# Eight slabs of modulation weights between the expert stage and the second block

## The chip, the cores and the metric

The kernel runs on one core of a Trainium2 chip. A core has a matrix engine (TensorE, PE in the profile; its weight loads are PEld), a vector engine (VectorE, DVE), a scalar engine (ScalarE, ACT), a general one (GpSimd, POOL) and a synchronizing one (SyncE, SP), which issues the DMA transfers here. Each engine carries out its own stream of instructions in order; semaphores tie the streams together. The metric is device time in microseconds of one execution, the median over runs.

## The reference, cut to what matters

The first block (a mixer with four branches, a layer norm, sixteen experts of which two serve a token, a second layer norm) is followed by a second block of two layers. Each layer has three sublayers, and each of them is scaled, shifted and gated by a modulation that comes from one conditioning vector:

```python
cond = jax.nn.silu(c)
for i in range(DEPTH_2):
    mod = cond @ ada_w[i] + ada_b[i]
    sh0, sc0, g0, sh1, sc1, g1, sh2, sc2, g2 = jnp.split(mod, N_MOD, axis=-1)
    h = modulate(rmsnorm(x, pre_norm[i, 0]), sh0, sc0)
    y = swiglu(h, ffn_w_gate[i, 0], ffn_w_up[i, 0], ffn_w_down[i, 0])
    x = x + FFN_HALF * g0[:, None, :] * rmsnorm(y, post_norm[i, 0])
    h = modulate(rmsnorm(x, pre_norm[i, 1]), sh1, sc1)
    ...  # y = dsa_mixer(h, ...) for i = 0, diff_mixer(h, ...) for i = 1
    x = x + g1[:, None, :] * rmsnorm(y, post_norm[i, 1])
    h = modulate(rmsnorm(x, pre_norm[i, 2]), sh2, sc2)
    ...  # a second swiglu, gated by g2
```

The width is 1024, there are 256 tokens. `cond @ ada_w[i]` is a product of one row with a matrix of 1024 x 9216 in fp32, 36 MB for each layer: little arithmetic, much to fetch.

## The kernel before

**Order of the work.** The mixer ends near 415 us, its norm and the router near 440. The experts run in eight pairs (`moe`) to about 685. At their end stands `overflow`, code for a token count above the capacity, behind a `tc.If` (L1515): a branch that every engine comes to. After it two matmul groups scatter the last pair's outputs into the result banks `y` (L1463), and the second layer norm follows, one half of 128 tokens at a time: `layer_norm` (L1165) as `ln2(0)`, `prenorm` (L327), then `ln2(1)` and its `prenorm`. `ln2w` is the normalized half; eight transposes `xp` (L350) turn it, and `xTf` is the result. Then `second` runs six steps (layer i, sublayer v): FFN(0,0), DSA(0,1), FFN(0,2), FFN(1,0), diff(1,1), FFN(1,2). The second half's head overlaps the first half's matmuls.

**Weights.** The class `Weights` holds one fixed list of slabs of 1 MB (`plan`). `pump` issues their transfers on SP strictly in that order, each as soon as a buffer of a fitting tag is free; `_raw_tag` picks the tag, the one whose buffers came free longest ago. A "split" slab is cut into a high part (ACT, L125) and a low part (DVE, L126), each in eight instructions of 256 columns, and PE multiplies with both: three passes (L276 to L278). A "raw" slab is used as it came, as the experts' are and the first FFN's first two slabs (`y<-xTf,rex` at L1596). From `second` on four buffers hold arriving slabs (one `rex`, three `raw`). During the experts more buffers serve (`wex`, `whi`, `wlo`, `wez`, `wea`).

**Modulation slabs.** `second_slabs` puts "ada" slabs among the weights. A group (layer i, sublayer v) has twelve of them: three column parts s (shift, scale, gate) of four slabs c. When the list's turn comes, `Ada.side` works a slab in. If the group is marked "vec", DVE multiplies and adds it into `asum` (L2138, L2140), two instructions of 1024 columns, and after four slabs PE sums `asum` over its partitions with a column of ones (8 records). If not, PE takes the slab itself (`rowsum`, L2146): four matmuls for each of its two blocks of 128 rows, which the profile records as 16. `drain` copies the sums out of the bank `adacc` on DVE (`aev`, one buffer, L2160) and sends them to row tiles by four transfers on SP (`arow`, L2163).

Before the change FFN(0,0), FFN(0,2) and FFN(1,0) carry 16, 16 and 12 vec slabs, DSA and diff 8 slabs each that are not vec, FFN(1,2) none. In DSA the eight stand behind the seven input slabs and ahead of the output slabs `dsa_w_out`; in diff three stand among the twelve input slabs and five behind them.

**What orders the instructions.** The scheduler of the framework writes each engine's stream from dependences, program order and its own estimate of times; `behind(tc, chain)` keeps a piece of code after the named instructions. Fillers such as the slab sums so come into gaps of that estimate.

Of the kernel before, what the change touches and what calls it, by code (L numbers as in the profile page):

```python
# [11 lines left out]
F32 = mybir.dt.float32  # L12
# [7 lines left out]
P = 128  # L20
T = 256
D = 1024
KC = D // P
# [5 lines left out]
@contextmanager  # L29
def behind(tc, chain):  # L30
    with ExitStack() as c:
        for i in chain:
            c.enter_context(tc.issue_after(i))
        yield


class Weights:
# [24 lines left out]
        self.hist[tag] = []  # L62

    def _raw_tag(self, j):
        order = ("wey", "wex", "rex", "b4", "raw", "whi", "wlo", "wez", "wea", "x") if self.slabs[j][0] == "raw" else ("rex", "raw")
        if any(s[0] == "split" for s in self.slabs[self.next_split:j]):
            order = [t for t in order if t not in ("whi", "wlo")]
        return min((t for t in order if self.bufs[t]), key=self._age)
# [114 lines left out]
    def _take(self):  # L183
        i = self.pos
        self.pos += 1
        kind, parts, a, b = self.slabs[i][:4]
        self.n_used += kind == "split"
        self.low = max(self.low, i if self.held is None else self.held)
        self.pump()
        if kind == "split":  # L190
            return [q[:, :a * b].rearrange("p (a b) -> p a b", a=a) for q in self.split.pop(i)]
        t = self.raw.pop(i)
        if kind == "raw":
            t = t if isinstance(t, list) else [t[:, :a * b].rearrange("p (a b) -> p a b", a=a)]
            return [v[:, c] for v in t for c in range(v.shape[1])]
        return t[:, :a * b].rearrange("p (a b) -> p a b", a=a)


def interleave(main, side, a, b):
    out, n = [], 0  # L200
    for i, m in enumerate(main):
        out.append(m)
        while n < len(side) and i + 1 > a + (b - a) * n / len(side):
            out.append(side[n])
            n += 1
    return out + side[n:]
# [120 lines left out]
def prenorm(k, t, x, xn, scr):  # L327
    ss = sums(k)
    for j, js in enumerate(HALVES):
        square(k, x[:, t, js], scr, ss, j)  # L330
    return scaled(k, t, x, ss, xn)
# [1222 lines left out]
def ffn_slabs(wg, wu, wd):  # L1554
    out = []
    for f0 in range(0, LAST, 256):
        two = [cols_slab(wg, f0, f0 + 256), cols_slab(wu, f0, f0 + 256)]
        out += [keep(v) for v in two] if f0 == 0 else two
    g, u = (w.rearrange("(k p) n -> p k n", p=P) for w in (wg, wu))
    out.append(("split", [((0, KC, 0, P + HALF), g[:, :, LAST:]), ((0, KC, P + HALF, 2 * P), u[:, :, LAST + P:])], KC, 2 * P))  # L1560
    out.append(cols_slab(wu, LAST, LAST + P))
    for r0, r1 in down_order():
        out.append(rows_slab(wd, r0, r1))
    return out
# [141 lines left out]
def dsa_slabs(w_in, w_out):  # L1706
    return proj_slabs(w_in, [1536, 1280, 1024] + list(range(0, 1024, 256))) + [rows_slab(w_out, r, r + 256) for r in range(0, D, 256)]


def diff_slabs(w_in, w_out):  # L1710
    return proj_slabs(w_in, range(0, 3072, 256)) + [rows_slab(w_out, r, r + 256) for r in range(0, D, 256)]
# [348 lines left out]
NR = 3 * D // P  # L2060


class Ada:
# [41 lines left out]
        nc.scalar.activation(self.cond, self.cols[:, 96:104], AF.Silu)  # L2105

    def acc_tile(self, t):
        self.acc = t[:, :T]
        self.k.nc.vector.memset(self.acc, 0.0)

    def slabs(self, li, v, vec):
        self.order.append((li, v))
# [4 lines left out]
            out += [("ada", [((0, 2, 0, D), w[c, :, :, c0:c0 + D])], 2, D, (li, v, vec, s, c)) for c in range(KC // 2)]  # L2117
        return out

    def side(self, meta, raw):  # L2120
        nc = self.k.nc
        self.drain()
        li, v, vec, s, c = meta
        name = li, v
        if s == c == 0:
            self.rows[name] = self.pool.tile([NR, P], F32, name="arow", tag="arow", bufs=3)
            self.bias[name] = self.pool.tile([NR, P], F32, name="ab", tag="ab", bufs=3)
            nc.sync.dma_start(out=self.bias[name], in_=self.a["ada_b_2"][li].rearrange("(v r c) -> v r c", v=3, c=P)[v])
        if vec and c == 0:
            self.sum = self.k.hp.tile([P, D], F32, name="asum", tag="asum", bufs=1)  # L2130
        with behind(self.k.tc, self.k.W.after if vec else []):
            for q in range(2):
                kc = 2 * c + q
                cond = self.cond[:, kc:kc + 1]
                if not vec:
                    self.rowsum(cond, raw[:, q], kc == 0, kc == KC - 1)
                elif kc == 0:
                    nc.vector.tensor_scalar(self.sum, raw[:, q], cond, None, op0=OP.mult)  # L2138
                else:
                    nc.vector.scalar_tensor_tensor(self.sum, raw[:, q], cond, self.sum, op0=OP.mult, op1=OP.add)  # L2140
        if c == KC // 2 - 1:
            self.flush = name, s, vec
            if s == 2:
                self.todo.append(name)
# [61 lines left out]


ENDS, END2 = (28, 28), 28
CSIDE, XSIDE, YSIDE = 3, 4, 4


def second_slabs(a, A):
    out = []
    ada = {n: A.slabs(*n, n[1] < 2) for n in ((0, 1), (0, 2), (1, 0), (1, 1), (1, 2))}
    vec = lambda slabs: [v[:4] + (v[4][:2] + (True,) + v[4][3:],) for v in slabs]
    sides = [(ada[0, 1] + vec(ada[0, 2][:4]), ada[0, 2][4:], ada[1, 0] + ada[1, 1][:YSIDE]),
             (ada[1, 1][YSIDE:] + vec(ada[1, 2][:XSIDE]), ada[1, 2][XSIDE:], [])]
    for i in range(2):
        f = [ffn_slabs(a["ffn_w_gate_2"][i][j], a["ffn_w_up_2"][i][j], a["ffn_w_down_2"][i][j]) for j in range(2)]
        if i == 0:  # L2220
            m, n = dsa_slabs(a["dsa_w_in_2"][0], a["dsa_w_out_2"][0]), 7
        else:
            m, n = diff_slabs(a["diff_w_in_2"][0], a["diff_w_out_2"][0]), 12
        s, c = sides[i], (0, CSIDE)[i]
        out += interleave(f[0], s[0], 2, ENDS[i])
        out += interleave(m[:n], s[1][:c], 2, n) + s[1][c:] + m[n:]
        out += interleave(f[1], s[2], 2, END2)
    return out
# [82 lines left out]
def tile_kernel(ctx, tc, a, out):  # L2311
    nc = tc.nc
    e = ctx.enter_context
    k = Kern(tc)
# [7 lines left out]
    A = k.A = Ada(k, a)  # L2322
# [7 lines left out]
    x = new_x()  # L2330
# [12 lines left out]
    b4, moe_ctx = ExitStack(), ExitStack()  # L2343
# [30 lines left out]
    with moe_ctx as c:  # L2374
# [47 lines left out]
        x, gb, scr = moe(k, c, a, new_x, *flat, yps, R, k.act)  # L2422
        w = k.act.tile([P, 2, D], F32, name="ln2w", tag="xTl", bufs=1)

        def ln2(t):
            return layer_norm(k, x[:, t], w[:, t], scr, x[:, t], [yps(t, 0), yps(t, 1)], 1.0 / ALPHA, gb[:, 0], gb[:, 1], x[:, t])[1]

        k.chain0 = [ln2(0)]
        xn = [prenorm(k, 0, x, w[:, 0], scr)]
        with behind(tc, k.chain):  # L2430
            ln2(1)
        xn.append(prenorm(k, 1, x, w[:, 1], scr))
    k.tmp = e(tc.tile_pool(name="tmp", bufs=1))
    with behind(tc, k.chain0):
        A.acc_tile(k.bank([P, 512], "adacc"))
    xT = Act3()
    xT.h, xT.l = pair([P, KC, T], F32R)
    xT.f = k.tmp.tile([P, KC, T], F32, name="xTf", tag="xTf", bufs=1)
# [22 lines left out]
```

## Time and profile before

| | us |
|---|---|
| median of three runs | 1732.62 (1730.42 to 1734.5) |
| the profiled execution | 1734.04 |
| its span, first to last instruction | 1732.3 |
| PE busy in it | 1676.4 (97%) |
| DVE busy | 1122.9 (65%) |
| ACT busy | 836.2 (48%) |

The times in the rows below are from the profiled execution and count from its first instruction. A window's row gives start, end, length, and for PE, PEld, DVE, ACT and POOL the busy time with the number of instructions in brackets, then the granted clock of PE (1.00 is the higher of its two levels), the mean busy share of the DMA engines and the GB/s moved. Shares of the whole span are averages over stages with different limits, so most rows are of a stage or of a few microseconds.

### The profile page before, as it was taken

Reading aid. Unit: us, or ns where it says so; the run is one execution under the profiler, and the core shown is the slowest. Engines: PE = TensorE matmul, PEld = TensorE weight load, DVE = VectorE, ACT = ScalarE, POOL = GpSimd, SP = SyncE. Lnnn points to the kernel's source line nnn. Section 1 sums busy time; section 2 is a strip of 40 time slices with the busy share of each in tenths; the row PEclk is TensorE's granted clock in tenths of the full one; section 3 lists DMA queues with packets and bytes.
Section 4 is the critical chain, followed back from the end, with each engine's and each line's share of the span. In section 5 each row is a group of like instructions: output and inputs, shape, how many; then the busy total and the mean of one; then the engine's idle time right before and its main releaser. Section 6 shows DMA issues by size and latency. Waiting matters only on the chain.

```text
span 1732.3 us, 30933 instructions
## 1 busy us (share of the span) xinstructions
PE 1676.4 (97%) x11786; PEld 1412.0 (82%) x11786; DVE 1122.9 (65%) x3100; ACT 836.2 (48%) x2367; POOL 28.3 (2%) x61
## 2 busy tenths in 40 slices
PE   7999999999899997999999999999999999999998
PEld 6998999998534443899878599988999778889986
DVE  5776676666521112888859788895977576786563
ACT  5446594344211111555644755563655475656552
POOL 1000011010000000000000000000000000000000
PEclk9999999999999999899999999999999999999999
DMA  6334657459999996599834659893988656347550
GB/s 209 122 122 147 194 177 236 149 182 353 353 390 395 395 392 251 174 308 302 318 107 149 245 189 312 288 346 118 325 259 274 223 188 218 130 145 250 174 204 25
DMA packets 247267, 404.35 MB, mean 233 GB/s; under 512 B 16271, under 2 KB 167478, under 8 KB 247110
## 3 DMA queue, kind: packets, MB, share of 16 engines
q1 hardware_dynamic: 247110, 402.29, 67.6%
q8 instruction: 95, 1.56, 0.4%
q14 instruction: 62, 0.51, 0.1%
HBM read 401.11 MB, written 1.07 MB: 232 GB/s over the span
## 4 chain that ended last, share of the span: by engine, by line
PE 51%; DVE 6%; ACT 2%; DMA 1%; issue 1%; DVEq 0%; ACTq 0%
PE y L276 5%; PE y L278 5%; PE y L277 5%; PE psg L276 4%; PE psg L277 4%; PE psg L278 4%; PE psu L276 4%; PE psu L278 4%; PE psu L277 4%; PE y L1596 2%; PE pj L277 1%; PE adacc L2148 1%; PE pj L276 1%; PE pj L278 1%; DVE wlo L126 1%; ACT scr L288 1%
## 5 line engine op out<-in xcount | busy, mean ns | idle before, releaser
L125 ACT ACTIVATE whi<-raw 128x256 fp32r<-128x256 f32 (+1 forms) x1005 | 330.0, 406 | 231.8 <-PE psmm L277 68.0
L126 DVE TENSOR_TENSOR wlo<-raw,whi 128x256 fp32r<-128x256 f32 (+1 forms) x1005 | 368.6, 425 | 103.6 <-ACT whi L125 103.2
L276 PE MATMUL psmm<-xTh,whi 128*128 128x256 f32 x584 | 170.6, 292 | 7.0 <-DVE gdn_k L592 5.1
L277 PE MATMUL psmm<-xTl,whi 128*128 128x256 f32 x584 | 167.6, 287 | 0.0
L278 PE MATMUL psmm<-xTh,wlo 128*128 128x256 f32 x584 | 167.4, 287 | 0.0
L276 PE MATMUL psg<-xTh,whi 128*128 128x256 f32 x560 | 159.0, 284 | 0.0
L278 PE MATMUL psg<-xTh,wlo 128*128 128x256 f32 x560 | 158.4, 283 | 0.0
L277 PE MATMUL psg<-xTl,whi 128*128 128x256 f32 x560 | 158.4, 283 | 0.0
L126 DVE TENSOR_TENSOR wlo<-rex,whi 128x256 fp32r<-128x256 f32 x296 | 104.1, 417 | 28.9 <-ACT whi L125 28.5
L125 ACT ACTIVATE whi<-rex 128x256 fp32r<-128x256 f32 x296 | 97.1, 405 | 52.9 <-PE y L278 15.4
L276 PEld LDWEIGHTS psmm<-xTh,whi 128*128 128x128 f32 x584 | 112.1, 192 | 12.0 <-ACT whi L125 7.2
L278 PEld LDWEIGHTS psmm<-xTh,wlo 128*128 128x128 f32 x584 | 112.1, 192 | 0.6
L277 PEld LDWEIGHTS psmm<-xTl,whi 128*128 128x128 f32 x584 | 112.1, 192 | 0.5
L276 PE MATMUL psu<-xTh,whi 128*128 128x256 f32 x392 | 111.0, 283 | 0.0
L277 PE MATMUL psu<-xTl,whi 128*128 128x256 f32 x392 | 110.9, 283 | 0.0
L278 PE MATMUL psu<-xTh,wlo 128*128 128x256 f32 x392 | 110.9, 283 | 0.0
L276 PEld LDWEIGHTS psg<-xTh,whi 128*128 128x128 f32 x560 | 107.4, 192 | 1.3 <-issue 1.3
L277 PEld LDWEIGHTS psg<-xTl,whi 128*128 128x128 f32 x560 | 107.4, 192 | 0.0
L278 PEld LDWEIGHTS psg<-xTh,wlo 128*128 128x128 f32 x560 | 107.4, 192 | 0.0
L276 PE MATMUL y<-whi,hh 128*128 128x512 f32 x264 | 105.5, 400 | 0.0
L278 PE MATMUL y<-whi,hl 128*128 128x512 f32 x264 | 104.5, 396 | 0.0
L277 PE MATMUL y<-wlo,hh 128*128 128x512 f32 x264 | 104.4, 395 | 0.0
(696 smaller groups left out, 4057.0 us busy)
## 6 DMA issues: line engine op xcount, KB each, us to landing
raw<-in_ada_w_dram SPq DMA_DIRECT2D x60, 1024.0 KB
raw<-in_w_in_dram SPq DMA_DIRECT2D x39, 1024.0 KB
raw<-in_ffn_w_up_dram SPq DMA_DIRECT2D x33, 1024.0 KB
raw<-in_ffn_w_down_dram SPq DMA_DIRECT2D x28, 1024.0 KB
raw<-in_ffn_w_gate_dram SPq DMA_DIRECT2D x27, 1024.0 KB
rex<-in_ffn_w_gate_dram SPq DMA_DIRECT2D x13, 1024.0 KB
rex<-in_ada_w_dram SPq DMA_DIRECT2D x12, 1024.0 KB
rex<-in_ffn_w_down_dram SPq DMA_DIRECT2D x12, 1024.0 KB
```

What stands on the lines that cost most here:

```text
L125: nc.scalar.activation(hi[:, c0:c1], t[:, c0:c1], AF.Copy)
L126: nc.vector.tensor_tensor(lo[:, c0:c1], t[:, c0:c1], hi[:, c0:c1].bitcast(F32), op=OP.subtract)
L276: nc.tensor.matmul(out, lh, rh, start=start, stop=False)
L277: nc.tensor.matmul(out, lh, rl, start=False, stop=False)
L278: nc.tensor.matmul(out, ll, rh, start=False, stop=stop)
L288: k.nc.scalar.activation(scr[:, HALVES[j]], v, AF.Square, scale=(RS / D) ** 0.5, accum_out=ss[:, j:j + 1])
L1596: nc.tensor.matmul(ps[c][:, i], raw[i][:, kc, c * P:(c + 1) * P], xT.f[:, kc, ts], start=kc == 0, stop=kc == KC - 1)
L2148: self.k.nc.tensor.matmul(self.acc[32 * c:32 * c + 1], col, v[:, c * T:(c + 1) * T], start=start, stop=stop, tile_position=(0, 32 * c))
```

## The change

Eight of the twelve slabs of group (0,1), its parts shift and scale, get the kind "gap" and come into the list right behind the experts' weights, ahead of the first FFN's. Their transfers go into `wex`, `whi`, `wlo`, `wez` and `wea`. Behind `moe` and ahead of `ln2(0)` the program takes them and sums them on PE (`gap`, 64 matmuls, 128 records) into the two halves of one bank `adacc`, which is cleared beforehand. After the second half's `prenorm`, behind the chain `k.chain`, `gap_drain` fetches the bias and drains both halves one after the other (two evictions, eight row transfers).

What the eight made room for moves forward: FFN(0,0) carries the rest of (0,1) and all of (0,2), 16 vec slabs as before; DSA carries none; FFN(0,2) as before; FFN(1,0) carries 16 vec slabs, four more; diff carries four slabs that are not vec, all behind its twelve input slabs.

```diff
--- before.py
+++ after.py
@@ -62,7 +62,8 @@
         self.hist[tag] = []
 
     def _raw_tag(self, j):
-        order = ("wey", "wex", "rex", "b4", "raw", "whi", "wlo", "wez", "wea", "x") if self.slabs[j][0] == "raw" else ("rex", "raw")
+        order = {"raw": ("wey", "wex", "rex", "b4", "raw", "whi", "wlo", "wez", "wea", "x"),
+                 "gap": ("wex", "whi", "wlo", "wez", "wea")}.get(self.slabs[j][0], ("rex", "raw"))
         if any(s[0] == "split" for s in self.slabs[self.next_split:j]):
             order = [t for t in order if t not in ("whi", "wlo")]
         return min((t for t in order if self.bufs[t]), key=self._age)
@@ -190,7 +191,7 @@
         if kind == "split":
             return [q[:, :a * b].rearrange("p (a b) -> p a b", a=a) for q in self.split.pop(i)]
         t = self.raw.pop(i)
-        if kind == "raw":
+        if kind in ("raw", "gap"):
             t = t if isinstance(t, list) else [t[:, :a * b].rearrange("p (a b) -> p a b", a=a)]
             return [v[:, c] for v in t for c in range(v.shape[1])]
         return t[:, :a * b].rearrange("p (a b) -> p a b", a=a)
@@ -2105,8 +2106,9 @@
         nc.scalar.activation(self.cond, self.cols[:, 96:104], AF.Silu)
 
     def acc_tile(self, t):
-        self.acc = t[:, :T]
-        self.k.nc.vector.memset(self.acc, 0.0)
+        self.both = t[:, :T], t[:, T:2 * T]
+        self.acc = self.both[0]
+        self.k.nc.vector.memset(t, 0.0)
 
     def slabs(self, li, v, vec):
         self.order.append((li, v))
@@ -2117,15 +2119,34 @@
             out += [("ada", [((0, 2, 0, D), w[c, :, :, c0:c0 + D])], 2, D, (li, v, vec, s, c)) for c in range(KC // 2)]
         return out
 
+    def open(self, name):
+        li, v = name
+        self.rows[name] = self.pool.tile([NR, P], F32, name="arow", tag="arow", bufs=3)
+        self.bias[name] = self.pool.tile([NR, P], F32, name="ab", tag="ab", bufs=3)
+        self.k.nc.sync.dma_start(out=self.bias[name], in_=self.a["ada_b_2"][li].rearrange("(v r c) -> v r c", v=3, c=P)[v])
+
+    def gap(self, slabs):
+        for (kind, parts, a, b, (li, v, vec, s, c)), raw in slabs:
+            self.acc = self.both[s]
+            for q in range(2):
+                kc = 2 * c + q
+                self.rowsum(self.cond[:, kc:kc + 1], raw[q], kc == 0, kc == KC - 1)
+
+    def gap_drain(self, name):
+        self.open(name)
+        for s in range(2):
+            self.acc = self.both[s]
+            self.flush = name, s, False
+            self.drain()
+        self.acc = self.both[0]
+
     def side(self, meta, raw):
         nc = self.k.nc
         self.drain()
         li, v, vec, s, c = meta
         name = li, v
         if s == c == 0:
-            self.rows[name] = self.pool.tile([NR, P], F32, name="arow", tag="arow", bufs=3)
-            self.bias[name] = self.pool.tile([NR, P], F32, name="ab", tag="ab", bufs=3)
-            nc.sync.dma_start(out=self.bias[name], in_=self.a["ada_b_2"][li].rearrange("(v r c) -> v r c", v=3, c=P)[v])
+            self.open(name)
         if vec and c == 0:
             self.sum = self.k.hp.tile([P, D], F32, name="asum", tag="asum", bufs=1)
         with behind(self.k.tc, self.k.W.after if vec else []):
@@ -2206,14 +2227,15 @@
 
 
 ENDS, END2 = (28, 28), 28
-CSIDE, XSIDE, YSIDE = 3, 4, 4
+CSIDE, XSIDE, YSIDE, GAP = 0, 8, 4, 8
 
 
 def second_slabs(a, A):
     out = []
-    ada = {n: A.slabs(*n, n[1] < 2) for n in ((0, 1), (0, 2), (1, 0), (1, 1), (1, 2))}
+    ada = {n: A.slabs(*n, n != (1, 2)) for n in ((0, 1), (0, 2), (1, 0), (1, 1), (1, 2))}
+    A.gaps = [("gap",) + v[1:] for v in ada[0, 1][:GAP]]
     vec = lambda slabs: [v[:4] + (v[4][:2] + (True,) + v[4][3:],) for v in slabs]
-    sides = [(ada[0, 1] + vec(ada[0, 2][:4]), ada[0, 2][4:], ada[1, 0] + ada[1, 1][:YSIDE]),
+    sides = [(ada[0, 1][GAP:] + ada[0, 2], [], ada[1, 0] + ada[1, 1][:YSIDE]),
              (ada[1, 1][YSIDE:] + vec(ada[1, 2][:XSIDE]), ada[1, 2][XSIDE:], [])]
     for i in range(2):
         f = [ffn_slabs(a["ffn_w_gate_2"][i][j], a["ffn_w_up_2"][i][j], a["ffn_w_down_2"][i][j]) for j in range(2)]
@@ -2222,6 +2244,8 @@
         else:
             m, n = diff_slabs(a["diff_w_in_2"][0], a["diff_w_out_2"][0]), 12
         s, c = sides[i], (0, CSIDE)[i]
+        if i == 0:
+            out += A.gaps
         out += interleave(f[0], s[0], 2, ENDS[i])
         out += interleave(m[:n], s[1][:c], 2, n) + s[1][c:] + m[n:]
         out += interleave(f[1], s[2], 2, END2)
@@ -2425,14 +2449,17 @@
         def ln2(t):
             return layer_norm(k, x[:, t], w[:, t], scr, x[:, t], [yps(t, 0), yps(t, 1)], 1.0 / ALPHA, gb[:, 0], gb[:, 1], x[:, t])[1]
 
+        acc = k.bank([P, 512], "adacc")
+        A.acc_tile(acc)
+        A.gap([(v, k.W._take()) for v in A.gaps])
         k.chain0 = [ln2(0)]
         xn = [prenorm(k, 0, x, w[:, 0], scr)]
         with behind(tc, k.chain):
             ln2(1)
         xn.append(prenorm(k, 1, x, w[:, 1], scr))
     k.tmp = e(tc.tile_pool(name="tmp", bufs=1))
-    with behind(tc, k.chain0):
-        A.acc_tile(k.bank([P, 512], "adacc"))
+    with behind(tc, k.chain):
+        A.gap_drain((0, 1))
     xT = Act3()
     xT.h, xT.l = pair([P, KC, T], F32R)
     xT.f = k.tmp.tile([P, KC, T], F32, name="xTf", tag="xTf", bufs=1)
```

## Rows read from the trace of the kernel before

**Rows 1.** Windows by stage (DSA, FFN(0,2), FFN(1,0), diff): busy us of each engine, then clock.

```profile
888.50:1018.29 129.79, 123.06 (x865) 94.12 (x865) 105.31 (x381) 75.73 (x229) 0.50 (x2) 1.00 0.47 163
1018.29:1211.27 192.98, 192.78 (x1375) 177.45 (x1375) 154.50 (x373) 103.28 (x305) 0.00 (x0) 1.00 0.78 268
1211.27:1404.91 193.64, 193.33 (x1350) 176.45 (x1351) 145.65 (x372) 104.94 (x306) 0.50 (x2) 1.00 0.73 246
1404.91:1545.09 140.18, 134.04 (x1021) 117.69 (x1018) 99.05 (x342) 83.50 (x286) 0.00 (x0) 0.99 0.55 185
```

**Rows 2.** The same view, 5 us windows at the end of the MoE.

```profile
670.00:675.00 5.00, 5.00 (x24) 2.38 (x20) 1.17 (x2) 0.38 (x1) 0.00 (x0) 1.00 1.10 364
...
690.00:695.00 5.00, 0.00 (x0) 0.00 (x0) 3.94 (x17) 1.51 (x5) 0.00 (x0) 0.50 0.00 0
```

**Rows 3.** Timeline of SP's queue, 640 to 720: start, us, line, transfer.

```profile
667.92 1.53 SPq L109 DMA_DIRECT2D raw<-in_ada_w_dram  x1
...
713.05 0.40 SPq L109 DMA_DIRECT2D rex<-in_ffn_w_up_dram  x1
```

**Rows 4.** Timelines of PE and ACT, 682 to 712; in brackets idle time before.

```profile
696.34 1.97 PE L350 MATMUL xp<-ident,ln2w 128*128 128x128 f32 x8 [11.18 <-ACT ln2w L337]
698.10 1.13 PE L1596 MATMUL y<-xTf,rex 128*128 128x128 f32 x4
...
707.55 1.04 PE L350 MATMUL xp<-ident,ln2w 128*128 128x128 f32 x8
...
705.63 0.72 ACT L337 ACTIVATE ln2w<-x,r 128x512 f32<-128x512 f32 x1 [1.50 <-DVE r L271]
```

**Rows 5.** Timeline of PE in diff: the records of one slab.

```profile
1493.35 1.04 PE L2148 MATMUL adacc<-raw,cond 128*1 128x256 f32 x16
```

**Rows 6.** Instructions of L1515, the branch: duration ns, first and last start.

```profile
L1515 SPq EVENT_SEMAPHORE  x8: 17/17/17, 675.9 to 678.1; - x8
...
L1515 SPq COMPARE_BRANCH  x1: 50/50/50, 670.2 to 670.2; - x1
...
L1515 DVEq COMPARE_BRANCH  x1: 76/76/76, 683.7 to 683.7; - x1
L1515 DVEq EVENT_SEMAPHORE  x1: 21/21/21, 686.7 to 686.7; - x1
```

**Rows 7.** DSA's two halves by windows: all engines, then `adacc` alone.

```profile
946.04:966.34 20.30, 19.22 (x181) 9.34 (x179) 12.58 (x47) 13.66 (x46) 0.00 (x0) 1.00 0.67 258
966.34:996.00 29.66, 28.10 (x171) 17.50 (x170) 27.08 (x70) 22.88 (x74) 0.00 (x0) 1.00 0.53 181
...
946.04:966.34 20.30, 9.54 (x98) 2.43 (x98) 0.42 (x1) 1.00 0.67 258
966.34:996.00 29.66, 2.15 (x31) 0.62 (x30) 0.42 (x1) 1.00 0.53 181
```

**Rows 8.** Chain of waits in DSA (`adacc` pieces), and timeline of ACT there.

```profile
947.07 0.52 PE adacc L2148 x2
...
974.86 0.54 PE adacc L2148 x6
...
950.23 1.28 ACT L1913 ACT_TABLE_LOAD   x1 [2.47 <-DVE mx L1910]
...
959.33 0.39 ACT L1913 ACTIVATE sm<-sm,mx 128x128 f32<-128x128 f32 x1
```

**Rows 9.** Diff: pieces of the chain of waits, and PE's waits.

```profile
1410.52 1.08 DVE wlo L126 x3
...
1415.14 8.65 DMA raw<-in_diff_w_in_dram
...
1441.37 0.95 PE adacc L2148 x10
...
PE dqt L1971 <- ACT wex L125: 1.4, 1, 1.4
PE dqt L1971 <- DVE difkq L1774: 1.1, 1, 1.1
```

## Prediction

> **What bounds the kernel now.** I read the busy time by stage first, because the change moves work between stages. In both FFN stages around the layer border PE is busy all but 0.2 to 0.3 us, with DVE at 154.50 of 192.98 and 145.65 of 193.64 [rows 1]: there PE sets the time. In the DSA stage PE is busy 123.06 of 129.79, in diff 134.04 of 140.18 [rows 1]: also near full, but these stages run a chain through DVE and ACT and use single-slab sums on PE as filler, so I must not count every PE record there as time.
>
> Then the end of the MoE in short windows. DMA still moves 364 GB/s at 670 to 675, and nothing at 690 to 695, when PE is empty too and its granted clock is 0.50, the lower of the two levels [rows 2]. The queue's own rows say how long that hole is: the last weight transfer is issued at 667.92 and the next at 713.05 [rows 3]. PE's timeline gives the other half: 11.18 us idle before the transposes of the first normalized half at 696.34 [rows 4]. So the change moves work into a real hole of DMA and of PE.
>
> Last the chain of waits in both attention stages, for what the filler costs where it is.
>
> **The head: eight slabs behind the MoE.** DMA: eight slabs of 1.05 MB at 364 GB/s are 2.9 us each, 23 in all. The FFN's first gate slab now queues behind them. What is in the queue before ends near 676.6 (an estimate: 667.92 and three slabs). Its last four slabs are three of the first FFN's and one ada slab, which now stand behind the eight. So the gate slab, ninth in the new queue, ends near 676.6 - 4 x 2.9 + 9 x 2.9 = 691, and the next, which PE wants later, at 694. PE reads the first at 698.10 [rows 4]. Slack 7 us: no cost.
>
> PE: 16 records of a slab that run back to back take 1.04 us [rows 5], eight take 8.4. They fit into the 11.18 us, if they stand behind the expert outputs and ahead of 696.34. Cost nothing; without that cover they cost at most 8.4.
>
> Clock: with PE busy in the hole, the lower clock may not come. The first half's eight transposes take 1.97 us at it, the second half's 1.04 [rows 4]: 0.9, and the matmuls behind them run faster too. But the second half's transposes cannot start before their `ln2w` is written (705.63 + 0.72 [rows 4]), and they started at 707.55: 1.2 us is the most. I take -1.2.
>
> The branch around the overflow code costs every engine time there. SP's branch at 670.2 is followed by its next event at 675.9, 5.7 us, while DMA is full; DVE's branch comes at 683.7, when the queue has run dry, and its next event at 686.7, 3.0 us later [rows 2, 6]. The layer norm starts behind that event. After the change DMA is full there too. If DVE's wait takes SP's length, +2.7, and all behind it shifts: layer norm, transposes, FFN. Bounds 0 and +2.7; I take +2.7, since SP's is the only row under load. The Trainium skill ("Runtime: NRT & Kernel Launch", section "Instruction fetch mechanics") says that a taken branch whose target lies outside the fetched pages forces a DMA fetch before the engine goes on; these rows agree that the engine stands still after its branch, and it speaks against this change, since that fetch would share DMA with the slabs. By it the head is +2.7 before the clock, without it 0.
>
> Drain: two evictions and eight row transfers. The transfers lie in SP's pause [rows 3], which is 45 us long; the second eviction waits for the first's rows (one buffer), and DVE's next work would stand behind it. 0 to +2; they are placed behind the norm's chain, so I take +0.3. Head: -1.2 + 2.7 + 0.3 = **+1.8**, bounds -1.2 and +4.7.
>
> **FFN stages.** FFN(0,0) and FFN(0,2) keep 16 slabs each. FFN(1,0) goes from 12 to 16 slabs summed on DVE. FFN(0,2) shows what 16 cost: 192.98 us, against 193.64 with 12 [rows 1]. PE gains one more flush of 8 records, half of 1.04: **+0.5**, bounds -0.7 and +0.5. DVE's four slabs hide behind PE (it has 48 us spare).
>
> **DSA: eight slabs fewer.** Their records keep PE busy 9.54 us in the first half and 2.15 in the second, 11.7 in all [rows 7]. On the chain of waits they have 11 pieces, 8.85 us, the first and the last of them here [rows 8]. ACT's exponentials of the first half run from 950.23, after a table load of 1.28 us, without a gap to 959.7 [rows 8], so the four pieces beside them (2.68, 0.97 and twice 0.52) cannot give time back. Ahead of them stand two pieces, 1.1 us; behind them up to 966.34 four pieces, 2.6; in the second half one, 0.5. That is 4.2. In the second half DVE is full, 27.08 of 29.66 [rows 7]. The output weights, which stood behind the eight slabs in the queue, now come earlier, so one slab's DVE split (eight subtractions at 0.36 us, 2.9, by the chain's piece of three [rows 9]) moves into the first half, where DVE has room: 12.58 of 20.30. Sum 4.2 + 2.9 = **-7.1**. Bounds: -3.1 (only the pieces behind the exponentials count) and -11.7 (all of PE's time).
>
> **Diff: four slabs instead of eight.** All four now stand behind the twelve input slabs instead of three among them. The chain waits 8.65 us for an input slab issued at 1415.14, but PE idles there only 1.4 + 1.1 us [rows 9]; with no ada slab ahead in the queue that slab comes a slab (2.9 us) sooner: -2.5. Two pieces of the slabs' records stand on the chain with 0.95 us each [rows 9]; half goes: -1.0. Together **-3.5**. Bounds: -1.0, and -4.4 (2.5 and both pieces).
>
> **Sum.** +1.8 + 0.5 - 7.1 - 3.5 = -8.3. The profiled execution took 1734.0 (its span and 1.7 us around it), so 1725.7; the median of the runs is 1.4 lower, so **1724.3**.
>
> **Rivals.** *All of PE's time returns.* 11.7 us in DSA, 4.2 in diff plus its wait of 2.5, +0.5 in FFN, head at +1.8 to 0: -16 to -18, 1716. For it: PE is 95% busy in both stages [rows 1]. Against it: the exponentials that cover a part.
>
> *Fewer fillers only open idle time.* The attention stages are then set by softmax on ACT and DVE: DSA -3.1, diff -1.0, head +1.8, FFN +0.5: -1.8, 1730.8. For it: ACT without a gap, DVE at 27 of 30 [rows 7, 8].
>
> *The first FFN weights come late (slower).* If the gap transfers are held until the buffers' last readers behind the branch have run, the first is issued near 686.7, when DVE leaves it [rows 6], and the ninth slab ends at 686.7 + 9 x 2.9 = 712.8, 14.7 behind 698.10. With -10.1 elsewhere and the head's +1.8: +6.4, 1739. It costs from the moment at which the first gap transfer starts later than 672.0, and outweighs the rest from 680 on. Against it: before, 1 MB slabs are issued as late as 667.92, ahead of SP's branch at 670.2, into buffers that pair 7 frees [rows 3, 6].
>
> **How the numbers follow.** My sum 0.60, with 1720 to 1729 as its own range (DSA -3 to -10, head -1 to +4, rarely together); all of PE's time 0.12; only idle time 0.18; late weights 0.10. The range 1717 to 1732 leaves out the late weights and half of the first rival. A measurement tells 0.2%, 3.5 us, from no change: faster means below 1729.2. The sum (0.57 of its 0.60), the first rival and 0.03 of the second: 0.72. Slower: late weights and 0.02 of the others, 0.12. The rest 0.16.
>
> **What the profile after would show.** Head: DMA full to about 698, 128 records of `adacc` between 685 and 697, the granted clock at 1.00 there, DVE's wait at the branch near 5.7, `xp` between 696 and 699. FFN(1,0): PE still full, 193 to 194.5 us. DSA: the stage at 121 to 125 us, no `adacc` on its chain, exponentials starting near the same distance from the stage's start. Diff: 135 to 138 us, PE's waits at `dqt` gone. It is wrong if PE waits for the DMA of the first gate slab, if the gap's records run after 697 or ahead of the expert outputs, or if the DSA stage keeps its length with PE idle instead.

## The result and the profile after

The changed kernel takes 1748.26 us (four runs, 1746.45 to 1748.72) against 1731.71 for the kernel before (four runs, 1730.42 to 1734.50): a ratio of 1.0093, interval 1.008 to 1.0105, so 16.5 us slower. The forecast was 1724.3, faster.

Stage by stage, measured in the profiled executions from the first transposes `xp` of the second half of one step to those of the next. "Head" is the stretch from the start of the scatter matmuls ahead of the last pair's second products to `xp` of the second half, so that it does not depend on how long the MoE took before:

| us | head | FFN(0,0) | DSA | FFN(0,2) | FFN(1,0) | diff |
|---|---|---|---|---|---|---|
| before | 35.5 | 193.3 | 116.2 | 193.0 | 193.3 | 140.4 |
| after | 38.7 | 193.3 | 117.7 | 193.0 | 197.8 | 148.4 |
| difference | +3.2 | 0 | +1.5 | 0 | +4.5 | +8.0 |

These sum to 17.2. The two spans differ by 14.5 only, because the profiled execution of after reached the scatter at 669.31 and that of before at 672.09. First the windows of DSA, FFN(1,0) and diff of after, as in [rows 1] (DSA's starts at the first half's head, the others at the second half's):

```profile
888.90:1019.80 130.90, 116.10 (x737) 93.48 (x736) 102.80 (x376) 75.59 (x228) 0.50 (x2) 0.92 0.30 97
...
1212.80:1410.60 197.80, 194.60 (x1344) 177.19 (x1343) 155.57 (x380) 105.16 (x307) 0.50 (x2) 0.99 0.77 262
1410.60:1559.10 148.50, 135.24 (x973) 120.73 (x971) 99.61 (x342) 84.11 (x286) 0.00 (x0) 0.95 0.44 146
```

The column behind the engines, PE's granted clock, tells most. In DSA the mean granted clock fell from 1.00 to 0.92, in diff from 0.99 to 0.95. PE's busy time in DSA fell by 7 us and the stage did not get shorter; in diff PE has 48 records fewer in its window (973 for 1021) and is busy 1.2 us longer.

**The head.** The branch's instructions and PE's timeline, of after (as [rows 6] and [rows 4]):

```profile
L1516 DVEq COMPARE_BRANCH  x1: 76/76/76, 680.9 to 680.9; - x1
...
L1516 DVEq EVENT_SEMAPHORE  x1: 21/21/21, 686.9 to 686.9; - x1
```

```profile
669.31 1.20 PE L1464 MATMUL y<-ys,GT 128*128 128x512 f32 x4
...
687.75 1.89 PE L2169 MATMUL adacc<-wez,cond 128*1 128x256 f32 x16 [3.05 <-DVE adacc L2111]
...
697.12 1.09 PE L351 MATMUL xp<-ident,ln2w 128*128 128x128 f32 x8
700.25 0.71 PE L1597 MATMUL y<-xTf,rex 128*128 128x128 f32 x4 [2.03 <-ACT xTf L357]
...
707.99 1.04 PE L351 MATMUL xp<-ident,ln2w 128*128 128x128 f32 x8
```

And PE's timeline of before at the anchor:

```profile
672.09 1.20 PE L1463 MATMUL y<-ys,GT 128*128 128x512 f32 x4
```

DVE stands 6.0 us between its branch and the next event instead of 3.0. The gap's sums run where they were expected, 687.75 to 697.1, and the first weights are there in time: the first FFN matmul waits for `xTf`, not for `rex`.

**DSA.** The windows of 10 us across the first half's softmax, and PE's longest waits in the stage, of after:

```profile
948.90:958.90 10.00, 4.33 (x30) 3.49 (x28) 10.00 (x40) 7.52 (x29) 0.00 (x0) 0.65 0.34 106
958.90:968.90 10.00, 6.40 (x24) 2.86 (x24) 7.10 (x26) 4.52 (x18) 0.00 (x0) 0.50 0.39 111
968.90:978.90 10.00, 8.69 (x46) 5.59 (x47) 5.69 (x9) 4.16 (x12) 0.00 (x0) 0.82 0.25 101
```

```profile
PE ppt L1922 <- DVE sm L1917: 4.8, 2, 2.8
PE po L1929 <- ACT pT L1927: 2.9, 4, 0.8
PE y L1833 <- DVE sm L1908: 2.8, 2, 2.1
```

PE's longest wait for `sm` in the stage before:

```profile
PE y L1832 <- DVE sm L1907: 0.9, 2, 0.7
```

Where the eight slabs' records had kept PE full, it is 43% busy and its clock falls to the lower level. DVE is full for ten microseconds, and its timeline shows with what (L127 is the split, L1910 is the softmax's maximum):

```profile
954.13 0.42 DVE L127 TENSOR_TENSOR wlo<-raw,whi 128x256 fp32r<-128x256 f32 x1
954.47 0.68 DVE L1910 TENSOR_REDUCE mx<-sm 128x4 f32<-128x512 f32 x1
955.06 0.41 DVE L127 TENSOR_TENSOR wlo<-raw,whi 128x256 fp32r<-128x256 f32 x1
```

Output weights are split between the softmax's own steps, and PE waits for `sm`. The second half's transposes `qt` start 81.6 us behind the stage's start instead of 76.3; the second half, now without splits and fillers, gives back 3.8 of these 5.3.

**FFN(1,0).** PE's longest wait there, SP's queue ahead of it and ACT's split that PE waits for, of after:

```profile
PE y L277 <- ACT whi L126: 1.7, 1, 1.7
```

```profile
1338.34 2.52 SPq L2184 DMA_DIRECT2D arow<-aev  x4
1340.96 2.58 SPq L110 DMA_DIRECT2D raw<-in_ffn_w_down_dram  x3
```

```profile
1346.02 4.26 ACT L126 ACTIVATE whi<-raw 128x256 fp32r<-128x256 f32 x13 [7.59 <-DMA raw<-in_ffn_w_down_dram]
```

Three transfers of `w_down` stand in SP's queue behind four row transfers, which wait for an eviction (`aev`) that DVE reaches at 1337.89, behind splits and FFN work. ACT's split waits 7.59 us for these weights, and PE runs dry behind it.

**Diff.** SP's first weight transfers in the stage, of before and of after, 15.1 and 18.6 us behind the first half's head (1389.9 and 1396.3), with the sums on PE of before that come just ahead of them:

```profile
1404.37 0.61 PE L2148 MATMUL adacc<-raw,cond 128*1 128x256 f32 x6
...
1405.03 4.01 SPq L109 DMA_DIRECT2D raw<-in_diff_w_in_dram  x2
```

```profile
1414.87 0.38 SPq L110 DMA_DIRECT2D raw<-in_diff_w_in_dram  x1
```

And the stretch between the two halves' attention, of after, as windows and as PE's longest wait of the stage:

```profile
1506.30:1511.30 5.00, 1.83 (x16) 1.29 (x16) 4.37 (x18) 4.00 (x16) 0.00 (x0) 1.00 0.60 199
1511.30:1516.30 5.00, 3.25 (x15) 3.25 (x16) 4.99 (x13) 2.57 (x8) 0.00 (x0) 0.55 0.01 4
```

```profile
PE dot L2042 <- DVE dO L2038: 5.2, 2, 4.9
```

PE is busy 1.83 us of five and then slow where slabs' records had stood. Before, the clock has a window at 0.66 at this place too (1499.9 to 1504.9, PE busy 4.57 of 5), and PE waits 2.0 us for `dO`.

### The profile page after: what moved, and what is told of

It is laid out like the page before. It is cut to its first block, busy times and chain, and to the rows that moved or that the text cites. A ratio compares the mean times of both kernels' runs of the same rounds, so it can differ in the third digit from the quotient of the medians.

```text
span 1746.8 us, 30833 instructions
## 1 busy us (share of the span) xinstructions
PE 1679.2 (96%) x11730; PEld 1416.9 (81%) x11730; DVE 1131.0 (65%) x3108; ACT 836.8 (48%) x2367; POOL 28.3 (2%) x61
## 4 chain that ended last, share of the span: by engine, by line
PE 49%; DVE 6%; DMA 3%; ACT 2%; issue 1%; SPq 0%; DVEq 0%; ACTq 0%
PE y L277 5%; PE y L278 5%; PE y L279 5%; PE psg L277 4%; PE psg L278 4%; PE psg L279 4%; PE psu L277 4%; PE psu L279 4%; PE psu L278 4%; PE y L1597 2%; DVE wlo L127 1%; PE adacc L2169 1%; PE pj L277 1%; PE pj L279 1%; PE pj L278 1%; ACT scr L289 1%
## 5 line engine op out<-in xcount | busy, mean ns | idle before, releaser
L127 DVE TENSOR_TENSOR wlo<-raw,whi 128x256 fp32r<-128x256 f32 (+1 forms) x1013 | 371.0, 425 | 101.8 <-ACT whi L126 100.2
L127 DVE TENSOR_TENSOR wlo<-rex,whi 128x256 fp32r<-128x256 f32 x288 | 101.3, 418 | 32.0 <-ACT whi L126 31.6
L126 ACT ACTIVATE whi<-rex 128x256 fp32r<-128x256 f32 x288 | 94.1, 405 | 50.5 <-issue 15.1
```

The source lines that it names most:

```text
L126: nc.scalar.activation(hi[:, c0:c1], t[:, c0:c1], AF.Copy)
L127: nc.vector.tensor_tensor(lo[:, c0:c1], t[:, c0:c1], hi[:, c0:c1].bitcast(F32), op=OP.subtract)
```

## The experiments

The theory after this reading: the transfers behind the MoE cost at the branch; in the attention stages the slabs had kept PE at its clock and the queue in a useful order; in FFN(1,0) the row transfers hold SP. The rivals stand with each run. In the edits, GAP is the number of slabs behind the experts, XSIDE the number of group (1,2)'s slabs that FFN(1,0) carries, and CSIDE the number of diff's slabs that stand among its input slabs. The table gives what all of them measured, by the same stages (medians of runs of the kernel before beside them: 1731.5 to 1733.1):

| us | head | DSA | FFN(1,0) | diff | median | ratio to before |
|---|---|---|---|---|---|---|
| gap_alone | 40.2 | 119.2 | 193.6 | 140.3 | 1736.7 | 1.0025 [1.0013, 1.0037] |
| gap_dma | 38.1 | 116.5 | 193.6 | 140.5 | 1735.9 | 1.0022 [1.0009, 1.0036] |
| dsa_only | 38.6 | 119.2 | 193.4 | 140.5 | 1740.7 | 1.0048 [1.0031, 1.0065] |
| dsa_fill | 38.6 | 117.8 | 193.6 | 141.7 | 1737.3 | 1.0030 [1.0020, 1.0040] |
| dsa_hold | 40.3 | 116.2 | 193.5 | 140.4 | 1735.2 | 1.0013 [1.0003, 1.0022] |
| dsa_fill_hold | 38.6 | 113.5 | 193.6 | 140.6 | 1732.5 | 1.0000 [0.9990, 1.0009] |
| layer1_only | 38.6 | 116.6 | 199.0 | 150.3 | 1747.9 | 1.0086 [1.0069, 1.0102] |
| layer1_order | 40.9 | 116.6 | 198.6 | 144.4 | 1746.4 | 1.0082 [1.0062, 1.0101] |
| diff_hold | 40.2 | 119.2 | 198.4 | 144.1 | 1745.6 | 1.0065 [1.0040, 1.0091] |
| diff_fill | 38.6 | 119.6 | 198.2 | 141.6 | 1741.7 | 1.0051 [1.0035, 1.0067] |
| layer1_arow | 38.6 | 116.5 | 194.4 | 144.6 | 1742.8 | 1.0064 [1.0042, 1.0086] |
| repaired | 40.2 | 116.2 | 194.4 | 141.8 | 1739.1 | 1.0035 [1.0022, 1.0049] |

The stage columns are of one execution each, and that execution lies up to 4.8 us from its kernel's median (`dsa_only` 4.0 below, `gap_alone` 3.9 and `dsa_hold` 3.8 above). Two of the columns have two values, and the rows show that PE's clock goes with them. Seven kernels of the table carry eight slabs in DSA as before. Four of them took 116.5 or 116.6 us there, with the clock at 1.00 in every window of 5 us; the three with 119.2 to 119.6 have two windows each at 0.66, 30 and 85 us behind the first half's head. The head takes 38.1 to 38.7 us where the clock is at 1.00 from 704 to 708, in the first FFN's matmuls, and 40.2 to 40.9 in the five kernels where it is at 0.57 to 0.61 there. The 4 us of `gap_alone`, and the second dip in its DSA stage:

```profile
704.00:708.00 4.00, 3.86 (x22) 3.80 (x22) 3.20 (x12) 2.23 (x6) 0.00 (x0) 0.59 0.01 4
...
976.90:981.90 5.00, 5.00 (x40) 1.96 (x39) 5.00 (x14) 3.35 (x13) 0.00 (x0) 0.66 0.12 16
```

Why the clock dips in some and not in others stays open; one profile of each kernel can't tell an execution from a program. So a difference of 2 to 3 us in these two columns needs the median and the clock beside it. The scheduler orders anew with every edit, so single microseconds can come from that too. FFN(0,0) took 191.8 with 8 slabs and 193.3 with 16.

**Which part costs what.** Four kernels undo parts of the change (with `sides` goes the line of `ada` of the kernel before); in `layer1_order` and the ones built on it the first layer is that of `gap_alone`.

```diff
 # gap_alone: FFN(0,0) 8 slabs, DSA 8; second layer as before
-CSIDE, XSIDE, YSIDE, GAP = 0, 8, 4, 8
+CSIDE, XSIDE, YSIDE, GAP = 3, 4, 4, 8
-    sides = [(ada[0, 1][GAP:] + ada[0, 2], [], ...
+    sides = [(ada[0, 1][GAP:] + vec(ada[0, 2][:4]), ada[0, 2][4:], ...
 # dsa_only: only the constants; layer1_only: only sides; layer1_order: sides and
+CSIDE, XSIDE, YSIDE, GAP = 3, 8, 4, 8
```

> The eight slabs behind the experts stay; what they free goes to the first FFN (8 slabs instead of 16), and DSA, FFN(1,0) and diff carry 8, 12 and 8 as in the kernel before. Theory (the head is harmless, the loss lies in the attention stages and FFN(1,0) losing or gaining slabs): head +0.4, two flushes of 0.54 less in FFN(0,0), so -0.7 us against before, 1731. Rival (the gap itself disturbs what follows, through buffers, the queue or the drain): +8 us or more, with DSA and diff longer although they carry what they carried.

> As the changed kernel up to FFN(0,2) (DSA without slabs), but FFN(1,0) with 12 and diff with 8 as before, three of these among the input slabs. Theory: each stage answers for itself, so head +0.4, DSA +1.5, rest 0: +1.9 us, 1733.6, with the granted clock at one half in DSA's first softmax. Rival (the whole loss follows from the empty DSA stage, by a shift of the queue that later stages pay): +14 us, 1746.

> FFN(0,0) 8 slabs, DSA 8 as before; FFN(1,0) 16 and diff 4 behind the input slabs, as in the changed kernel. Theory: head +0.4, two flushes less -1.1, FFN(1,0) +4.4, diff +8.1: +11.8 us, 1743.5. Rival (the second layer pays for what DSA leaves behind): +2 us or less.

> As layer1_only, but three of diff's four slabs stand among its input slabs as in the kernel before, and one behind. If the order in the queue is the loss in diff (a slab whose buffer comes free early lets the next input slab start 3.5 us sooner), some 6 of diff's 8.1 us come back: 1737. If the number of slabs as fillers is the loss, less than 2 come back: 1742 to 1744. FFN(1,0)'s 4.4 stay in both.

`gap_alone` came out 4.2 us slower than before where my theory said -0.7: the head is not harmless. In absolute times the early MoE of after's profile had hidden the 3.2 us; the stretch from the scatter shows them. The rest of the rival fell: FFN(1,0) and diff are as before. `dsa_only` is 4 us over `gap_alone` by the medians, 1.5 of it the longer FFN(0,0), and 8.3 over the kernel before where I had expected 1.9. Both layers answer for themselves: FFN(1,0) and diff stay at 193.4 and 140.5 there, and take 199.0 and 150.3 in `layer1_only` with the old DSA (15.5 us slower by the medians, 11.8 expected). In `layer1_order` the diff stage gives back 5.9 of 9.9 us, and its first weight transfers start 15.5 us behind the first half's head (1397.7) again, just behind a slab's sums on PE:

```profile
1412.49 0.61 PE L2169 MATMUL adacc<-raw,cond 128*1 128x256 f32 x6
...
1413.15 4.01 SPq L110 DMA_DIRECT2D raw<-in_diff_w_in_dram  x2
```

The reason is the buffer: a slab that PE sums at once frees its buffer before the first input slabs, which both halves use, free theirs. SP's transfer starts 0.05 us after the sums end, in before (1404.98) and here (1413.10). With four input slabs in the four buffers nothing can be fetched until PE is through with the first. FFN(1,0)'s loss stays, as expected.

The medians do not show these 5.9 us: 1747.9 and 1746.4 lie in each other's range, and neither the 1737 of the one theory nor the 1742 to 1744 of the other came. In the profiled executions the longer head of `layer1_order`, with its lower clock, takes 2.3 us of them back. So the gain rests on the stage alone, where it came again: 144.1 to 144.6 us in the three kernels with this order and no fillers (`layer1_order`, `diff_hold`, `layer1_arow`), 148.4 and 150.3 in the two without it (after and `layer1_only`).

**The head: transfers or matmuls.**

```diff
 # before_nobranch and gap_nobranch: the kernel before, and gap_alone, each with
-            overflow(k, a, cnti[0], pos, comb, x, ...)
 # gap_dma: gap_alone, in Ada.gap
...
-                self.rowsum(self.cond[:, kc:kc + 1], raw[q], kc == 0, kc == KC - 1)
+            pass
```

> The kernel before without the overflow code and its branch (the path for token counts above the capacity is left out; these inputs don't take it). It is the base for the next run. Each engine's stand at the branch (DVE's is 3.0 us) goes from the path: 2 to 4 us less than before under both theories, 1729.

> gap_alone without the overflow code and its branch. Theory (the +4 us of gap_alone are the branch: its fetch shares DMA with the eight slabs, DVE stands 6.0 us there instead of 3.0): without a branch the gap costs nothing and two flushes of 1.1 us are saved, so 0 to -2 us against before_nobranch. Rival (the gap costs through the memset, the evictions, the row transfers or buffers): +3 to +5 us against before_nobranch, as with the branch.

> gap_alone with the eight slabs' transfers but without their 64 matmuls (the sums of shift and scale of group (0,1) are left out). Anchor: from the start of the scatter matmuls ahead of the last pair's second products to the second half's transposes, 35.5 us before, 38.6 to 40.9 in the kernels with the gap. Theory (the transfers slow the fetch behind the branch): DVE stands 6 us at its branch as in all kernels with the gap, and the stretch is 39 to 41 us. Rival (the matmuls on PE, or what stands on DVE for them): DVE's stand goes back to 3 us and the stretch to 35 to 37.

`before_nobranch` took 1727.4 us against 1732.1, ratio 0.9971 [0.996, 0.9983]: the overflow code and its branch cost the kernel before some 5 us. `gap_nobranch` took 1738.2, 10.8 more, and its time does not answer the question: without the barrier the scheduler put the second half's transposes and the gap's last sums ahead of the first FFN's matmuls in PE's order, and FFN(0,0) took 202.6 us. PE's timeline of it:

```profile
690.10 1.97 PE L351 MATMUL xp<-ident,ln2w 128*128 128x128 f32 x8 [6.09 <-ACT ln2w L338]
...
701.05 1.97 PE L351 MATMUL xp<-ident,ln2w 128*128 128x128 f32 x8 [4.42 <-ACT ln2w L338]
...
706.31 3.84 PE L1590 MATMUL y<-xTf,rex 128*128 128x128 f32 x32
```

Both halves' transposes start where they start in `before_nobranch` (690.3 and 701.5): the head is 32.2 us against 32.5, so the norm itself lost nothing to the transfers there; the order did. `gap_dma` keeps the branch, leaves out the gap's matmuls and with them the sums of shift and scale, and settles it. The branch's instructions and PE's timeline of it:

```profile
L1516 DVEq COMPARE_BRANCH  x1: 76/76/76, 682.2 to 682.2; - x1
...
L1516 DVEq EVENT_SEMAPHORE  x1: 21/21/21, 688.3 to 688.3; - x1
```

```profile
670.58 1.20 PE L1464 MATMUL y<-ys,GT 128*128 128x512 f32 x4
...
708.71 1.04 PE L351 MATMUL xp<-ident,ln2w 128*128 128x128 f32 x8
```

Without a single matmul of the gap DVE stands 6.1 us, and the stretch is 38.1. The eight transfers are enough to double the stand at the branch. What the DMA queues carried during DVE's stand, of before (683.7 to 686.7) and of after (680.9 to 686.9), as packets, MB and share of the DMA engines:

```profile
q1 hardware_dynamic: 120, 0.29, 28.5%
q14 instruction: 3, 0.02, 2.6%
```

```profile
q1 hardware_dynamic: 1610, 2.17, 103.9%
q8 instruction: 1, 0.02, 1.4%
q14 instruction: 2, 0.02, 0.8%
```

Three instruction packets are moved in either stand, and in that of `gap_dma`, beside a share of 28.5% and 103.9% for data; from 675 to 690 `before_nobranch` has none, before has eight. The Trainium skill ("Runtime: NRT & Kernel Launch", section "Instruction fetch mechanics") says that a taken branch whose target lies outside the pages fetched ahead makes the engine wait until DMA has brought that page; the pair of stands, 3.0 and 6.1, and these packets agree, though no row shows which engine a packet was for.

**DSA: clock or order.**

```diff
 # dsa_fill: dsa_only, in the second half's loop over g (fill: a slab's matmuls on xT.f)
             if t:
-                k.W.side_some(NSIDE)
+                for f in range(NSIDE):
+                    fill()
 # dsa_hold: dsa_only; last is the first half's last exponential
     for c in range(0, 1024, 256):
+        k.W.splitting = c < 768
         proj_tm(k, xT, pj, c, 256)
...
+            if t == 0 and g == 3:
+                k.W.after, k.W.splitting = [last], True
+                k.W.pump()
 # dsa_fill_hold: both
```

> dsa_only with 64 matmuls on PE in DSA's softmax of the same shape as the eight slabs' had, on data that is there anyway, their sums unused; no transfer, no buffer. If the loss in DSA is PE's clock (its fillers kept it at 1.00), the clock stays at 1.00 and the stage falls by 2 us or more, to 117 or less between the heads of the second half. If the loss is the output weights' splits that now stand ahead of the softmax on DVE and ACT, PE still waits for sm and the stage stays within 1 us of dsa_only or grows: 119 to 121.

> dsa_only with the splits of DSA's output weights held until the last exponential of the first half is issued; no fillers. If these splits on DVE and ACT are the loss, PE's waits for sm (7.6 us in the changed kernel) fall to 2 us or less and the stage is 3 to 7 us shorter than in dsa_only: 112 to 116. If the clock is the loss, it falls to one half here too (PE is even emptier) and the stage stays at 118 to 121.

> dsa_only with both edits: 64 slab-like matmuls on PE (data that is there, sums unused) and the output weights' splits held behind the first half's exponentials. Against dsa_hold this adds PE's fillers, against the kernel before it lacks only the eight transfers. In dsa_hold the stage is 116.2 us between the heads of the second half, with the clock at 0.50 to 0.65 for 20 us. If the clock eats what the missing fillers would give, the stage falls to 113.5 to 115. If softmax on ACT and DVE sets it whatever PE does, it stays at 116 to 117.

The three as 10 us windows at the same place of the stage, 60 and 70 us behind its start: `dsa_fill`, `dsa_hold`, `dsa_fill_hold`.

```profile
948.60:958.60 10.00, 8.36 (x94) 4.23 (x94) 8.77 (x33) 6.53 (x25) 0.00 (x0) 0.83 0.35 109
958.60:968.60 10.00, 6.95 (x60) 2.72 (x59) 8.32 (x30) 5.70 (x21) 0.00 (x0) 1.00 0.34 104
```

```profile
953.30:963.30 10.00, 5.64 (x30) 3.73 (x32) 7.62 (x26) 7.55 (x29) 0.00 (x0) 0.65 0.00 1
963.30:973.30 10.00, 7.57 (x30) 3.88 (x28) 7.15 (x24) 7.95 (x27) 0.00 (x0) 0.50 0.19 57
```

```profile
948.50:958.50 10.00, 9.84 (x118) 4.97 (x114) 7.97 (x27) 7.11 (x27) 0.00 (x0) 1.00 0.01 2
958.50:968.50 10.00, 7.89 (x57) 4.49 (x53) 7.59 (x26) 9.39 (x33) 0.00 (x0) 0.84 0.26 76
```

With fillers alone the clock is back for most of the stretch and the stage is 117.8, between the two forecasts (117 or less, 119 to 121); PE's waits for `sm` are still 4.5 us. With the splits held alone the clock falls as in after and the stage is 116.2, no shorter than with eight slabs; PE's waits for `sm` fell from 7.8 us in `dsa_only` to 4.6, not to the 2 expected. With both they are 1.1 us and the stage is 113.5: holding the splits takes 4.3 us off `dsa_fill`, and 64 matmuls of no use take 2.7 off `dsa_hold`. The medians go the same way: 1740.7, 1737.3, 1735.2, 1732.5. So neither cause is the whole: the order of the splits hides the clock, and behind it the clock eats 2.7 us. (These matmuls do nothing that is needed, so what they give can only be the clock or a new order by the scheduler; the clock is what the windows show.) `dsa_fill_hold` brings the stage under the one before, and with the head's loss the kernel is level with before. No version that I ran beats the kernel before with the same work done.

**FFN(1,0) and what was left in diff.**

```diff
 # layer1_arow: layer1_order, in Ada.drain
-            nc.sync.dma_start(out=self.rows[name][r0:r0 + 2], ...
+            (nc.scalar if name[0] else nc.sync).dma_start(out=self.rows[name][r0:r0 + 2], ...
 # diff_hold: layer1_order; sq is the first half's last square
+                k.W.splitting = hp < 3
                 proj_tm(k, xT, vv, hp * 256, 256)
...
+        if t == 0 and hp == 3:
+            k.W.after, k.W.splitting = [sq], True
+            k.W.pump()
 # diff_fill: layer1_order, in the second half
                 k.W.side_some(DSIDE)
+                for f in range(2):
+                    fill()
```

> layer1_order with the row transfers of the second layer's sums issued by ACT instead of SP. In FFN(1,0) (198.6 us between the heads of the second half, 193.3 before) the output weights' transfers stand behind four row transfers in SP's order. If that is what starves PE, the stage falls to 195 or less. If it is that DVE reaches its slab sums late and so frees the buffers late, it stays within 1 us of 198.6.

> layer1_order with the splits of diff's output weights held until the first half's attention is through. In layer1_order the diff stage is 144.4 us between the heads of the second half (140.4 before), and the splits stand among the first half's softmax. If they are what is left of the loss, the stage falls to 140 to 142. If it is PE's emptiness in the second half (clock at 0.59 to 0.73 there, four slabs fewer), it stays at 144 or grows.

> layer1_order with 8 slab-like groups of matmuls on PE in the second half of diff's attention (data that is there, sums unused). If the lower clock is what is left of the loss, the stage falls to 141 to 142, with the granted clock at 1.00 in the stretch where it was 0.59 to 0.73. If it is DVE's order, PE still waits 5 us ahead of dot and the stage stays at 144 or above.

With ACT issuing the rows FFN(1,0) falls from 198.6 to 194.4, and PE has no wait for weights left there; the four kernels of the table with 16 slabs there and the rows on SP took 198.2 to 199.0. SP's queue and ACT's timeline of `layer1_arow`:

```profile
1334.85 8.56 SPq L110 DMA_DIRECT2D raw<-in_ffn_w_down_dram  x3
```

```profile
1336.05 2.35 ACTq L2184 DMA_DIRECT2D arow<-aev  x4
```

`w_down` no longer stands behind the rows. In diff the held splits changed nothing (144.1), the fillers gave 2.8 of the 4.0 that were left (141.6). The stretch between the halves in `diff_fill`, as far behind the first half's head as the two windows of after above:

```profile
1508.80:1513.80 5.00, 4.17 (x41) 2.82 (x37) 4.84 (x11) 2.38 (x8) 0.00 (x0) 1.00 0.02 3
1513.80:1518.80 5.00, 5.00 (x38) 4.50 (x38) 4.35 (x13) 2.85 (x14) 0.00 (x0) 1.00 0.00 1
```

The clock is 1.00 where it was 0.69 and 0.63 in `layer1_order`. PE's waits ahead of `dot`, 5.3 us there, are 1.1 us, in part because the dummy matmuls now fill them; so clock and order are not parted here as they are in DSA.

**The sum.** `repaired` is the changed kernel with the edits of `dsa_hold`, `layer1_arow` and `diff_fill`, and CSIDE = 3.

> The changed kernel with the four losses undone one by one where they arise: DSA's output splits held, the second layer's row transfers issued by ACT, three of diff's slabs among its input slabs, slab-like matmuls (data that is there, sums unused) in diff's second half. By the single runs: DSA -1.5, FFN(1,0) -4.2, diff -5.9 and -2.8, of the changed kernel's 1748.3: some 1735 to 1737, so 3 to 5 us over the kernel before, which is the head. If the losses share a cause, less than half of the 14 comes back: above 1741.

1739.1 us, 6.1 more than the kernel before in the runs beside it, where the changed kernel had 16.5 more: 10.4 us come back. By stages it is +4.8 in the head, 0 in DSA, +1.1 in FFN(1,0) and +1.4 in diff against before, 7.3 in all. The head is the one with the lower clock. I had expected 1735 to 1737: DSA gave its 1.5, but FFN(1,0) and diff gave 10.0 where the single runs had promised 12.9. These 12.9 were counted down from `layer1_only` (199.0 and 150.3), 3.1 us above the changed kernel (197.8 and 148.4). The stages end where the single runs had brought them, at 194.4 and 141.8 (194.4 in `layer1_arow`, 141.6 in `diff_fill`), so nothing here shows that the losses share a cause.

## Why the prediction was wrong

**The head (+1.8, measured +3.2): right in mechanism, too small.** DVE's stand was forecast at 5.7 us and is 6.0: the term of +2.7 is +3.0, and `gap_dma` shows its cause. The term of -1.2 for the clock is the one that failed. The clock did rise: eight transposes take 1.09 us instead of 1.97, and from the first FFN matmul to the second half's transposes it is 7.7 us instead of 9.5. But from DVE's event to those transposes it takes 21.1 us after and 20.9 before, because what lies ahead of that matmul grew as much. The first transposes start 0.6 us later behind the event: the memset of `adacc`, 0.48 us, now stands ahead of the norm on DVE. And the matmul starts 3.1 us behind them instead of 1.8: ACT writes its first `xTf` at 699.76, behind the first activations of the second half's norm, where before it did so at 697.49, ahead of it. The slack of the first FFN weights held; the rival of late weights did not come.

**FFN(1,0) (+0.5, measured +4.5): wrong.** "FFN(0,2) shows what 16 cost" compared numbers of slabs and not places in SP's queue. DVE's capacity was indeed there; but a late eviction held four row transfers, and behind them on SP three slabs of `w_down`. The part that the issuing engine decides measured 4.2 us.

**DSA (-7.1, measured +1.5): wrong, and in both terms.** The step "one slab's split moves into the first half, where DVE has room" took busy time for room: some three slabs' splits moved, and stood between the softmax's steps on the engine that PE was waiting for. Its 2.9 us of gain became a loss of 4.3 (`dsa_fill` against `dsa_fill_hold`). The term of 4.2 for filler pieces off the chain assumed that the rest of PE's work keeps its speed. It does not: once the fillers are gone the clock falls to the lower level for some 20 us. With the splits out of the way and the clock kept the stage is 2.7 us under before, but with as many matmuls on PE as before; what the pieces off the chain are worth at the higher clock no run shows. The prediction's own sign of being wrong, that the stage keeps its length with PE idle instead, is what came.

**Diff (-3.5, measured +8.0): wrong.** The step "with no ada slab ahead in the queue that slab comes a slab sooner" had the sign reversed: the ada slab was what freed a buffer early, and without it the next input slab starts 3.4 us later. That is the larger part, 4.0 us from after to `layer1_order` and 5.9 from `layer1_only`. The smaller part, 2.8 us, came back with the fillers and with them PE's clock. Some 1 us of diff is left open, as in FFN(1,0).

**The rivals.** "Fewer fillers only open idle time" (1730.8) was the nearest in mechanism; it counted the idle time at nothing and left out what PE's clock does in it. The rival for slower (1739) was the nearest in time and the only one with the right sign, but by luck: it named the wrong transfers, and the first FFN weights were never late. All of PE's time returning was furthest off.

## What to carry to other kernels

Work that fills an engine's gaps may have three side effects that its busy time does not show: in this kernel it kept the clock up, it freed buffers early, and it held other work back from an engine that was just then on the path. Before it is moved away, ask of each place what comes next in every queue when it is gone. And small transfers that wait for an eviction stand in the same queue as the weights behind them; a free place in DMA says nothing about the place in the queue.

## What the runs showed of the hardware

The overflow code, which these inputs do not need, and its branch cost the kernel before some 5 us (1732.1 against 1727.4 without them). DVE's stand at the branch goes from 3.0 to 6.0 us when data fills the DMA engines beside it (103.9% instead of 28.5%). I had not expected the fillers to matter so much for the clock: in DSA's first softmax PE was 43% busy in one window of 10 us and the granted clock was 0.65 there and 0.50, the lower level, in the next; with dummy matmuls and held splits (98% and 79% busy) it was 1.00 and 0.84. The clock also dipped to 0.66 for 5 us in windows in which PE was busy throughout (`gap_alone`, 976.9 to 981.9), in some kernels and not in others, and each pair of such dips goes with some 3 us of the DSA stage.
